# Gathering two heads of a cached page with one indirect transfer, and scoring the new key apart

## The chip, the cores and the metric

The kernel runs on one core of one Trainium2 chip. The metric is device time in microseconds (us) of one execution: the median of three executions, with the lowest and the highest beside it. A reading of 0.2% or less is about what a measurement of this kernel cannot tell from no change.

## The reference, cut to what matters

One layer of a decoder works on 256 prompt tokens and on 8 samples with one new token each. Everything is float32. A projection of 2048 features feeds three branches; the change touches only the third, the attention of the 8 samples over a paged cache.

```python
PAGE_SIZE, PAST_LEN, N_KV, N_HEADS, HEAD_DIM = 128, 256, 4, 16, 128     # two pages for each sample
top_k = min(TOPK_MAX, (PAST_LEN + T) // 4)                              # 64 of 257 keys
pool_k = ck.reshape(-1, N_KV, HEAD_DIM)                                 # cache: page, position, kv head, feature
row = phys * PAGE_SIZE + pc % PAGE_SIZE                                 # phys: from the sample's page table
k_sel = jnp.where(is_past, pool_k[row], take_rows(k, ni))               # the 257th key is the new token's
qg = q.reshape(B, T, N_KV, N_HEADS // N_KV, HEAD_DIM)                   # 4 query heads share a kv head
s = jnp.einsum('btngd,btsnd->btngs', qg, k_sel) * HEAD_DIM ** -0.5
p = jax.nn.softmax(jnp.where(valid, s, -jnp.inf), axis=-1)
o = jnp.einsum('btngs,btsnd->btngd', p, v_sel)
```

The kernel computes the scores of all 257 keys of a sample and adds -1e30 to those that the indexer did not select, which gives the same softmax.

## The kernel before, in words

The 264 tokens are the moving operand of all large products, with features on the partitions. The work is a stream of feature tiles of 128 columns, in the order of a list (`ORDER`): the indexer's key, 4 tiles of k, 4 of v, 8 of the indexer's queries, 16 of `va`, 16 of `q` (one for each query head), 16 of `zc`, and the rest. A tile is 16 blocks of K; each block is three matmuls (L1010, `acc<-hh,wh`, `acc<-hl,wh`, `acc<-hh,wl`), since every float32 operand is carried as two parts, a high and a low one. ScalarE makes the high part of the weights (L157, `wh`), VectorE the low one (L160, `wl`). SyncE loads the weights in units of 512 KB into six buffers.

The order of the instructions on each engine is the order in which the program issues them: there is no scheduler. What follows a tile's product is a generator (`Tasks`): it yields the number of steps until it goes on, and a step is one unit of 24 matmuls of the stream, so a tile has two steps. Each engine takes its own instructions strictly in that order and waits by semaphores for the others.

The attention of the samples for kv head `n` (0 to 3) is `sample(n)`. It is spawned 3 steps after the last of the four query heads that share the kv head, and goes through five places, one step apart: the scores of the 8 samples (L726, `ssP`, 8 matmuls whose result is 32 rows by 257 columns, since a 32-row stretch of the result holds two samples); the softmax; its transposes (L736, `spT`); the product with the values (L746, `soP`, 16 matmuls of 32 x 128); the transpose back (L756, `soT`). In the trace a float32 matmul of this kind is two rows, so `ssP` has 16 and `soP` 32 for each `sample(n)`.

The keys and values come from HBM by indirect transfers that GpSimd issues (`gather`, L711 to L717): one for each sample, page and kv head, of 128 rows of 512 bytes, row numbers from `rows`. There are 16 for the keys and 16 for the values of one kv head, 128 in all. The buffers `gk` and `gv` hold two kv heads each: `top_k` issues the gathers of heads 0 and 1 (keys 0, values 0, keys 1, values 1), `sample(0)` and `sample(1)` issue those of heads 2 and 3 into the places that they have just read. The new token's key is copied into column 256 of `gk` by VectorE (L721).

Of the kernel before, what the change touches and what calls it, by code (L numbers as in the profile page):

```python
# [10 lines left out]
I32 = mybir.dt.int32  # L11
# [20 lines left out]
# first column of each part of w_in  # L32
# [3 lines left out]
# feature tiles of 128 columns in the order in which they are computed  # L36
# [9 lines left out]
# the first tiles are computed in parts of K, while the modulation of the later parts still comes in  # L46
# [3 lines left out]
# buffers of loads; units that are split ahead of their use (one, for the first NEAR loads), each in  # L50
# CUT parts; tiles over which the loads of the next piece's modulation are spread
# [7 lines left out]
def _mods():  # L59
    """The loads of w_mod, by piece of shift and scale or of the gate: columns for each k, the k,  # L60
    and where they are in the packed array."""
    out, off = [], 0
    for width in [256 * nk for _, nk in PIECES] + [128 * nk for _, nk in GATES]:
        per = max(1, 1024 // width)
        out.append([])
        for k in range(0, KB, per):
            out[-1].append((width, list(range(k, k + per)), off))
            off += width * per * P
    return out
# [5 lines left out]
def _stream():  # L75
    """The loads in the order in which they are used: ("m", piece, load) of w_mod, and ("w", n, parts)
    of the tiles' weights, eight blocks of 128 x 128 each, as (tile, first k block, k blocks)."""
    items, n = [("m", 0, i) for i in range(len(MODS[0]))], 0
    for q, (k0, nk) in enumerate(PIECES):
        ms = [("m", q + 1, i) for i in range(len(MODS[q + 1]))] if q + 1 < len(PIECES) else []  # L80
        done = 0
        for j in range(0, EARLY, 8 // nk):
            while done < len(ms) and done * MOD_BY <= j * len(ms):
                items.append(ms[done])
                done += 1
            items.append(("w", n, [(x, k0, nk) for x in range(j, j + 8 // nk)]))
            n += 1
        assert done == len(ms)
    gate = [("m", q, i) for q in range(len(PIECES), len(MODS)) for i in range(len(MODS[q]))]
    for j in range(EARLY, len(ORDER)):  # L90
        for k0 in (0, 8):
            items.append(("w", n, [(j, k0, 8)]))
            n += 1
            if gate and ORDER[j][0] in ("u", "za"):
                items.append(gate.pop(0))
    return items
# [4 lines left out]
# columns of the packed per-feature parameters, [128, KB] each unless said otherwise  # L101
# [4 lines left out]
class Tasks:  # L106
    """Work that follows a tile's product, spread over later steps: generators that yield the
    number of steps until they go on."""
# [21 lines left out]
def trunk_kernel(ctx: ExitStack, tc: tile.TileContext, a: dict, o: dict):  # L130
# [11 lines left out]
    def slot(name, dt=F32, shape=(P, KB, T)):  # L142
        return big.tile(list(shape), dt, name=name, tag="big")
# [28 lines left out]
    # the tensor engine's clock comes up before the first loads arrive  # L172
# [32 lines left out]
    def ctile(name, shape, dt=F32, bufs=1):  # L205
        return cp.tile(list(shape), dt, name=name, tag=name, bufs=bufs)

# [9 lines left out]
    rows = ctile("rows", [P, 5, 16], I32)  # L217
    rowf = ctile("rowf", [P, 16])
    dve.tensor_scalar(rowf, ptf, 128.0, pidx[:, 0:1], op0=OP.mult, op1=OP.add)
    for n in range(4):  # L220
        dve.tensor_scalar(rows[:, n, :], rowf, float(n * N_PHYS * P), None, op0=OP.add)
    dve.tensor_scalar(rows[:, 4, :], ptf, 64.0, pidx[:, 1:2], op0=OP.mult, op1=OP.add)

    # sel[b, r] = 1 where row r = 32 (b // 2) + 4 (b % 2) + h belongs to sample b
# [6 lines left out]
    # heads of the indexer on partitions, 16 b + h: a copy of the identity for each sample  # L231
# [21 lines left out]
    # the extra buffers are for the loads up to the last of shift and scale  # L253
# [27 lines left out]
    # the weights of the next units, up to the n-th from here on, in the two parts that float32r  # L281
    # carries
# [32 lines left out]
    # 1 / sqrt(x / D + EPS), with a step of Newton's behind ScalarE's square root  # L315
# [12 lines left out]
    # the same of the tokens' sums over the partitions, for every partition, in PSUM  # L328
# [36 lines left out]
    # 1 / rms of the tokens, for every partition  # L365
# [25 lines left out]
    # up to four groups of n columns, a tile of 32 columns of the tensor engine's for each  # L391
# [94 lines left out]
    def gather_kix():  # L486
        kix = S["kix"] = slot("kix", shape=(P, NS, KEYS))
        for b in range(NS):
            for g in range(PAGES):
                i = b * PAGES + g  # L490
                pool.indirect_dma_start(out=kix[:, b, g * P:(g + 1) * P], out_offset=None, in_=a["cidx"],
                                        in_offset=bass.IndirectOffsetOnAxis(ap=rows[:, 4, i:i + 1], axis=0))
# [62 lines left out]
    def post_qi(j, src):  # L555
# [5 lines left out]
        # a head's 64 rows in two parts that float32r carries, one above the other  # L561
# [28 lines left out]
    def top_k():  # L590
# [21 lines left out]
        S["gk"] = slot("gk", shape=(P, 2, NS, KEYS))  # L612
        S["gv"] = slot("gv", shape=(P, 2, NS * PAGES, P))
        for n in range(2):
            gather(n, "gk")
            gather(n, "gv")
# [47 lines left out]
    # prompt attention of one head; the samples' after the last head of a group  # L664
    def post_q(h, src):
# [8 lines left out]
        if hh4 == 3:  # L674
            tasks.spawn(sample(n), 3)
# [35 lines left out]
    def gather(n, what):  # L711
        for b in range(NS):
            for g in range(PAGES):
                i = b * PAGES + g
                to = S["gk"][:, n % 2, b, g * P:(g + 1) * P] if what == "gk" else S["gv"][:, n % 2, i, :]
                pool.indirect_dma_start(out=to, out_offset=None, in_=a["ck" if what == "gk" else "cv"],  # L716
                                        in_offset=bass.IndirectOffsetOnAxis(ap=rows[:, n, i:i + 1], axis=0))  # L717

    def sample(n):
        gk, gv = S["gk"], S["gv"]  # L720
        dve.tensor_copy(gk[:, n % 2, :, 256], kT[:, n, NP:T])  # L721
        yield 1
        p = pss("ssP")
        for s in range(2):
            for c in range(4):
                pe.matmul(p[32 * c:32 * c + 32, 0:KEYS], qpad[n % 2][:, c, 32 * s:32 * s + 32],  # L726
                          gk[:, n % 2, 2 * c + s, :], start=s == 0, stop=s == 1, skip_group_check=True)
        if n < 2:
            gather(n + 2, "gk")
# [13 lines left out]
        for s in range(2):  # L743
            for g in range(PAGES):
                for c in range(4):
                    pe.matmul(p[32 * c:32 * c + 32, 0:P], ppad[n % 2][:, g, c, 32 * s:32 * s + 32],  # L746
                              gv[:, n % 2, (2 * c + s) * PAGES + g, :], start=first, stop=s == 1 and g == 1,
                              skip_group_check=True)
                first = False
        if n < 2:  # L750
            gather(n + 2, "gv")
# [22 lines left out]
    # twice silu(z)  # L774
# [24 lines left out]
    # merged holds twice the sum  # L799
# [134 lines left out]
    # what has to be there before a tile's work  # L934
    def start_a():
# [21 lines left out]
        # the part of the samples' convolution that comes from their state  # L957
# [9 lines left out]
    # 4 log(sigmoid(x)) = 4 (min(x, 0) - 2 atanh(y / (2 + y))), y = exp(-|x|)  # L967
# [85 lines left out]
    # the prompt's rows come back to tokens on partitions, where 1 / rms is one factor for each  # L1053
# [40 lines left out]
def _layout(i):  # L1094
# [29 lines left out]
    def feat(x):  # L1124
# [13 lines left out]
        ck=i["cache_k"][0].transpose(2, 0, 3, 1).reshape(-1, P),  # L1138
        cv=i["cache_v"][0].transpose(2, 0, 1, 3).reshape(-1, P),
# [48 lines left out]
```

## Time and profile before

| | us |
|---|---|
| device time, median of 3 | 1746.52 (1745.45 to 1747.11) |
| span of the profiled execution, first to last instruction | 1614.2 |
| what lies around the span, by the median | 132.3 |
| TensorE busy with matmuls | 1578.5 (98% of the span) |
| VectorE, ScalarE, GpSimd busy | 990.1, 807.9, 295.5 |
| TensorE's mean granted clock | 0.990 of full speed |

The profile is of one execution. No device time of its own was kept for that execution, so the median of the three stands for it: 1746.5 = 1614.2 + 132.3. The 132.3 us are outside all the instructions of the program. Where the text speaks of kv head 0 it means the stretch at about 328 to 343 us of the span, of head 1 362 to 382, of head 2 402 to 422, and of head 3 442 to 464.

### The profile page before, as it was taken

Reading aid. Unit: us, or ns where it says so; the run is one execution under the profiler, and the core shown is the slowest. Engines: PE = TensorE matmul, PEld = TensorE weight load, DVE = VectorE, ACT = ScalarE, POOL = GpSimd, SP = SyncE. Lnnn points to the kernel's source line nnn. Section 1 sums busy time; section 2 is a strip of 40 time slices with the busy share of each in tenths; the row PEclk is TensorE's granted clock in tenths of the full one; section 3 lists DMA queues with packets and bytes.
Section 4 is the critical chain, followed back from the end, with each engine's and each line's share of the span. In section 5 each row is a group of like instructions: output and inputs, shape, how many; then the busy total and the mean of one; then the engine's idle time right before and its main releaser. Section 6 shows DMA issues by size and latency. Waiting matters only on the chain.

```text
span 1614.2 us, 33342 instructions
## 1 busy us (share of the span) xinstructions
PE 1578.5 (98%) x13289; PEld 1518.1 (94%) x13289; DVE 990.1 (61%) x2111; ACT 807.9 (50%) x1628; POOL 295.5 (18%) x411
## 2 busy tenths in 40 slices
PE   8999999998889999999999999999999999999998
PEld 7888899998879999998889999999999999999997
DVE  6876589754446645544546654444777777766654
ACT  5333368554435444443334444444777777754442
POOL 4000256577730001000000000000211111100011
PEclk9999999999989999999999999999999999999999
DMA  8898863655445555657885556555465545555652
GB/s 337 304 362 286 284 207 119 192 180 155 156 151 174 185 182 184 201 184 268 286 273 186 172 182 235 181 181 181 152 198 174 173 162 186 180 190 183 234 183 83
DMA packets 91867, 326.26 MB, mean 202 GB/s; under 512 B 12320, under 2 KB 12768, under 8 KB 91328
## 3 DMA queue, kind: packets, MB, share of 16 engines
q1 hardware_dynamic: 86608, 313.18, 57.4%
q0 software_dynamic: 5104, 10.96, 2.3%
q8 instruction: 104, 1.70, 0.4%
q14 instruction: 51, 0.42, 0.1%
HBM read 320.35 MB, written 3.67 MB: 201 GB/s over the span
## 4 chain that ended last, share of the span: by engine, by line
PE 70%; DVE 1%; issue 0%; POOL 0%; DMA 0%; ACT 0%; DVEq 0%; ACTq 0%
PE acc L1010 68%; PE pmod L407 1%; PE spP L838 0%; PE giP L879 0%; PE gaP L879 0%; POOL gv L716 0%; DVE x L161 0%; DVE ls L158 0%; DMA gv<-in_cv,rows 0%; DVE ls L981 0%; DVE wl L160 0%; PE rsP L1063 0%; DVE o L158 0%; DVEq L1154 0%; ACT wh L157 0%
## 5 line engine op out<-in xcount | busy, mean ns | idle before, releaser
L160 DVE TENSOR_TENSOR wl<-raw,wh 128x512 fp32r<-128x512 f32 x926 | 613.2, 706 | 371.9 <-ACT wh L157 352.8
L1010 PE MATMUL acc<-hh,wh 128*128 128x264 f32 x2832 | 822.5, 290 | 6.8 <-DVE part L159 2.6
L1010 PE MATMUL acc<-hh,wl 128*128 128x264 f32 x2832 | 805.1, 284 | 1.9 <-DVE wl L160 1.9
L1010 PE MATMUL acc<-hl,wh 128*128 128x264 f32 x2832 | 806.0, 285 | 0.1
L157 ACT ACTIVATE wh<-raw 128x512 fp32r<-128x512 f32 x926 | 530.3, 622 | 496.6 <-PE acc L1010 357.4
L1010 PEld LDWEIGHTS acc<-hh,wh 128*128 128x128 f32 x2832 | 536.6, 189 | 41.0 <-issue 25.1
L1010 PEld LDWEIGHTS acc<-hl,wh 128*128 128x128 f32 x2832 | 537.0, 190 | 0.7 <-DVE hl L160 0.4
L1010 PEld LDWEIGHTS acc<-hh,wl 128*128 128x128 f32 x2832 | 534.2, 189 | 2.3 <-DVE wl L160 2.3
L1010 PE MATMUL acc<-ah,wh 128*128 128x264 f32 x768 | 217.9, 284 | 0.0
L1010 PE MATMUL acc<-al,wh 128*128 128x264 f32 x768 | 217.6, 283 | 0.0
L1010 PE MATMUL acc<-ah,wl 128*128 128x264 f32 x768 | 217.4, 283 | 0.0
L1010 PEld LDWEIGHTS acc<-al,wh 128*128 128x128 f32 x768 | 144.7, 188 | 0.0
L1010 PEld LDWEIGHTS acc<-ah,wh 128*128 128x128 f32 x768 | 144.6, 188 | 0.0
L1010 PEld LDWEIGHTS acc<-ah,wl 128*128 128x128 f32 x768 | 144.0, 187 | 0.0
L810 POOL TENSOR_TENSOR mg<-mg,gp 128x264 f32<-128x264 f32 x16 | 12.0, 752 | 473.8 <-DVE gp L161 473.8
L159 DVE TENSOR_TENSOR part<-acc,part 128x264 f32<-128x264 f32 x128 | 51.6, 428 | 35.6 <-PE acc L1010 35.2
L1010 PE MATMUL acc<-mh,wh 128*128 128x264 f32 x256 | 72.6, 284 | 0.0
L1010 PE MATMUL acc<-ml,wh 128*128 128x264 f32 x256 | 72.5, 283 | 0.0
L1010 PE MATMUL acc<-mh,wl 128*128 128x264 f32 x256 | 72.5, 283 | 0.0
L716 POOL DMA_INDIRECT gk<-in_ck,rows x64 | 64.2, 1003 | 19.4 <-issue 16.3
L716 POOL DMA_INDIRECT gv<-in_cv,rows x64 | 62.1, 970 | 19.5 <-issue 18.3
L1010 PEld LDWEIGHTS acc<-ml,wh 128*128 128x128 f32 x256 | 48.2, 188 | 0.0
(377 smaller groups left out, 1266.8 us busy)
## 6 DMA issues: line engine op xcount, KB each, us to landing
raw<-in_wall SPq DMA_DIRECT2D x463, 512.0 KB, 3.7
raw<-in_wmod SPq DMA_DIRECT2D x73, 512.0 KB, 5.6
rawx<-in_wmod SPq DMA_DIRECT2D x23, 512.0 KB, 6.4
rawx<-in_wall SPq DMA_DIRECT2D x19, 512.0 KB, 6.0
xr<-in_xT SPq DMA_DIRECT2D x4, 528.0 KB, 5.6
wrg<-in_wrg SPq DMA_DIRECT2D x1, 2048.0 KB, 8.5
x<-in_xp SPq DMA_DIRECT2D x1, 2048.0 KB, 9.5
out_yp<-x SPq DMA_DIRECT2D x8, 256.0 KB, 2.4
```

The lines of the kernel that those rows point to most:

```text
L157: copy = lambda out, x, scale=1.0: act.activation(out, x, AF.Copy, scale=scale)
L159: add = lambda out, x, y: dve.tensor_tensor(out, x, y, OP.add)
L160: sub = lambda out, x, y: dve.tensor_tensor(out, x, y, OP.subtract)
L407: pe.matmul(MOD[q][32 * g:32 * g + 32, 0:n], cpad[:, k, :], r[:, c:c + n], start=k == 0, stop=k == KB - 1, skip_group_check=True)
L716: pool.indirect_dma_start(out=to, out_offset=None, in_=a["ck" if what == "gk" else "cv"], in_offset=bass.IndirectOffsetOnAxis(ap=rows[:, n ...
L810: pool.tensor_tensor(S["mg"][:, j, :], S["mg"][:, j, :], x, OP.add)
L1010: pe.matmul(c[:, 0:T], x[:, kk * P:(kk + 1) * P], y[:, k, :], start=n == 0 and (kk == 0 if early else k == 0), stop=n == 2 and (kk == nk - ...
```

## The change

One transfer now fetches both kv heads of a pair for a page: 128 rows of 1,024 bytes, for which the host lays out the caches with the two heads of a pair side by side. There are 16 gathers for the keys and 16 for the values of a pair, 64 in all. `gk` and `gv` hold one pair; `top_k` issues the gathers of pair 0 (heads 0 and 1), and `sample(1)` issues those of pair 1 (heads 2 and 3), the keys behind its scores and the values behind its product. The scores of the cached keys are matmuls of 256 columns; the new token's key no longer goes into `gk`, and its column of scores comes from 8 matmuls of one column for each kv head (32 more in all). `sample(2)` starts 5 steps behind its query head and no longer 3. Two of the five tables of row numbers go.

```diff
@@ indexer and attention: constants
-    rows = ctile("rows", [P, 5, 16], I32)
+    rows = ctile("rows", [P, 3, 16], I32)
...
-    for n in range(4):
-        dve.tensor_scalar(rows[:, n, :], rowf, float(n * N_PHYS * P), None, op0=OP.add)
+    for n in range(2):
+        dve.tensor_scalar(rows[:, n, :], rowf, 2.0, float(n), op0=OP.mult, op1=OP.add)
@@ top_k
-        S["gk"] = slot("gk", shape=(P, 2, NS, KEYS))
-        S["gv"] = slot("gv", shape=(P, 2, NS * PAGES, P))
-        for n in range(2):
-            gather(n, "gk")
-            gather(n, "gv")
+        S["gk"] = slot("gk", shape=(P, NS * PAGES, 2, P))
+        S["gv"] = slot("gv", shape=(P, NS * PAGES, 2, P))
+        gather(0, "gk")
+        gather(0, "gv")
@@ post_q
-            tasks.spawn(sample(n), 3)
+            tasks.spawn(sample(n), 5 if n == 2 else 3)
@@ gather, sample
-    def gather(n, what):
-        for b in range(NS):
-            for g in range(PAGES):
-                i = b * PAGES + g
-                to = S["gk"][:, n % 2, b, g * P:(g + 1) * P] if what == "gk" else S["gv"][:, n % 2, i, :]
-                pool.indirect_dma_start(out=to, out_offset=None, in_=a["ck" if what == "gk" else "cv"],
-                                        in_offset=bass.IndirectOffsetOnAxis(ap=rows[:, n, i:i + 1], axis=0))
+    def gather(pair, what):
+        for i in range(NS * PAGES):
+            pool.indirect_dma_start(out=S[what][:, i].rearrange("p n x -> p (n x)"), out_offset=None,
+                                    in_=a["ck" if what == "gk" else "cv"],
+                                    in_offset=bass.IndirectOffsetOnAxis(ap=rows[:, pair, i:i + 1], axis=0))
 
     def sample(n):
         gk, gv = S["gk"], S["gv"]
-        dve.tensor_copy(gk[:, n % 2, :, 256], kT[:, n, NP:T])
+        h = n % 2
         yield 1
         p = pss("ssP")
         for s in range(2):
             for c in range(4):
-                pe.matmul(p[32 * c:32 * c + 32, 0:KEYS], qpad[n % 2][:, c, 32 * s:32 * s + 32],
-                          gk[:, n % 2, 2 * c + s, :], start=s == 0, stop=s == 1, skip_group_check=True)
-        if n < 2:
-            gather(n + 2, "gk")
+                b = 2 * c + s
+                pe.matmul(p[32 * c:32 * c + 32, 0:NP], qpad[n % 2][:, c, 32 * s:32 * s + 32],
+                          gk[:, PAGES * b:PAGES * b + PAGES, h, :], start=s == 0, stop=s == 1,
+                          skip_group_check=True)
+        for s in range(2):
+            for c in range(4):
+                b = NP + 2 * c + s
+                pe.matmul(p[32 * c:32 * c + 32, NP:KEYS], qpad[n % 2][:, c, 32 * s:32 * s + 32],
+                          kT[:, n, b:b + 1], start=False, stop=s == 1, skip_group_check=True)
+        if n == 1:
+            gather(1, "gk")
...
-                              gv[:, n % 2, (2 * c + s) * PAGES + g, :], start=first, stop=s == 1 and g == 1,
+                              gv[:, (2 * c + s) * PAGES + g, h, :], start=first, stop=s == 1 and g == 1,
...
-        if n < 2:
-            gather(n + 2, "gv")
+        if n == 1:
+            gather(1, "gv")
@@ _layout (on the host)
-        ck=i["cache_k"][0].transpose(2, 0, 3, 1).reshape(-1, P),
-        cv=i["cache_v"][0].transpose(2, 0, 1, 3).reshape(-1, P),
+        ck=i["cache_k"][0].transpose(0, 3, 2, 1).reshape(-1, 2 * P),
+        cv=i["cache_v"][0].reshape(-1, 2 * P),
```

The change also takes the comments out of the file, which shifts the line numbers by a few.

On GpSimd's queue, from the last work on the mask of the prompt (`bias`) to the store of `gv` rows at the end of the gMLP's norm (`out_gv`), the rows before are these, 16 gathers to a row:

```order
L588 AFFINE_SELECT bias<-bias 128x256
L716 DMA gk<-in_ck,rows 128x128 x16
L716 DMA gv<-in_cv,rows 128x128 x16
L716 DMA gk<-in_ck,rows 128x128 x16
L716 DMA gv<-in_cv,rows 128x128 x16
L716 DMA gk<-in_ck,rows 128x128 x16
L716 DMA gv<-in_cv,rows 128x128 x16
L716 DMA gk<-in_ck,rows 128x128 x16
L716 DMA gv<-in_cv,rows 128x128 x16
L662 DMA out_gv<-vsr 128x128
```

and now:

```order
L589 AFFINE_SELECT bias<-bias 128x128
L590 AFFINE_SELECT bias<-bias 128x256
L715 DMA gk<-in_ck,rows 128x256 x16
L715 DMA gv<-in_cv,rows 128x256 x16
L715 DMA gk<-in_ck,rows 128x256 x16
L715 DMA gv<-in_cv,rows 128x256 x16
L663 DMA out_gv<-vsr 128x128
```

The values of head 1, which stood behind 48 other gathers, now come with those of head 0, behind 16; the last gather of all stands behind 63 others and no longer 127.

On TensorE's queue, the scores of kv head 0 (`ssP`), between the transposes of a query head of the prompt (`pT`) and the stream's next matmul (`acc`), were:

```order
L691 MATMUL oP<-et,vn 128x256
L693 MATMUL oP<-et,vn 128x128
L686 MATMUL pT<-ident,e 128x128 x3
L726 MATMUL ssP<-gk,qpad_169 32x257 x8
L1010 MATMUL acc<-hh,wh 128x264
```

and are now:

```order
L692 MATMUL oP<-et,vn 128x256
L694 MATMUL oP<-et,vn 128x128
L687 MATMUL pT<-ident,e 128x128 x3
L727 MATMUL ssP<-gk,qpad_167 32x256 x8
L733 MATMUL ssP<-kT,qpad_167 32x1 x8
L1017 MATMUL acc<-hh,wh 128x264
```

The eight matmuls of one column stand directly behind the eight of the cached keys; the same holds for the other three kv heads.

On TensorE's queue, the first nine rows of the product with the values of kv head 1 (`soP`) with the semaphores that they wait for (DMASW0 to DMASW7 are eight counters of GpSimd's transfers, taken in turn) were:

```order
L679 MATMUL sP<-kT,qt 128x256
L746 MATMUL soP<-gv,ppad_172 32x128 [waits DMASW6_49,DVE_49]
L746 MATMUL soP<-gv,ppad_172 32x128 [waits DMASW2_49]
L746 MATMUL soP<-gv,ppad_172 32x128 [waits DMASW6_49]
L746 MATMUL soP<-gv,ppad_172 32x128 [waits DMASW2_49]
L746 MATMUL soP<-gv,ppad_172 32x128 [waits DMASW7_49]
L746 MATMUL soP<-gv,ppad_172 32x128 [waits DMASW3_49]
L746 MATMUL soP<-gv,ppad_172 32x128 [waits DMASW7_49]
L746 MATMUL soP<-gv,ppad_172 32x128 [waits DMASW3_49]
L746 MATMUL soP<-gv,ppad_172 32x128 [waits DMASW0_49,DVE_49]
```

and all sixteen of them now are:

```order
L680 MATMUL sP<-kT,qt 128x256
L753 MATMUL soP<-gv,ppad_170 32x128 [waits DVE_49]
L753 MATMUL soP<-gv,ppad_170 32x128 x7
L753 MATMUL soP<-gv,ppad_170 32x128 [waits DVE_49]
L753 MATMUL soP<-gv,ppad_170 32x128 x7
L1017 MATMUL acc<-hh,wh 128x264
```

The products of heads 1 and 3 wait for no transfer of their own any more, since heads 0 and 2 have already waited for the same gathers.

## Rows read from the trace of the kernel before

**Rows 1.** The head of the page: the span, and each engine's busy time with its share of the span.

```profile
span 1614.2 us, 33342 instructions
PE 1578.5 (98%) x13289; PEld 1518.1 (94%) x13289; DVE 990.1 (61%) x2111; ACT 807.9 (50%) x1628; POOL 295.5 (18%) x411
```

**Rows 2.** TensorE's waits between 296 and 470 us: who waited for what, us in total, times, longest.

```profile
PE soP L746 <- DMA gv<-in_cv,rows: 15.3, 8, 5.0
```

**Rows 3.** TensorE's timeline at the four products with the values: start us, length us (of the whole run where there are several), line, operation, count, and in brackets the idle time before it with what ended it. First kv head 0, then 1, 2 and 3; each ends with the stream's first matmul behind the product, and with the first one that was started at the old pace again (the 18th, 19th and 14th from there).

```profile
341.37 1.08 PE L746 MATMUL soP<-gv,ppad 128*32 128x128 f32 x32
342.38 0.39 PE L1010 MATMUL acc<-hh,wh 128*128 128x264 f32 x1
342.60 0.28 PE L1010 MATMUL acc<-hl,wh 128*128 128x264 f32 x1
...
374.58 0.42 PE L746 MATMUL soP<-gv,ppad 128*32 128x128 f32 x6
...
381.12 0.59 PE L1010 MATMUL acc<-hh,wh 128*128 128x264 f32 x1
...
385.09 0.29 PE L1010 MATMUL acc<-hh,wh 128*128 128x264 f32 x1
...
415.05 0.42 PE L746 MATMUL soP<-gv,ppad 128*32 128x128 f32 x6
...
421.59 0.59 PE L1010 MATMUL acc<-hh,wh 128*128 128x264 f32 x1
...
425.91 0.29 PE L1010 MATMUL acc<-hl,wh 128*128 128x264 f32 x1
...
453.08 0.57 PE L746 MATMUL soP<-gv,ppad 128*32 128x128 f32 x6
458.70 0.66 PE L746 MATMUL soP<-gv,ppad 128*32 128x128 f32 x8 [5.05 <-DMA gv<-in_cv,rows]
...
463.67 0.59 PE L1010 MATMUL acc<-hh,wh 128*128 128x264 f32 x1
...
466.88 0.28 PE L1010 MATMUL acc<-hh,wl 128*128 128x264 f32 x1
```

**Rows 4.** The chain of work that ended last, in order of time (start us, length us, what): the end of the gathers and the stretch of TensorE behind them.

```profile
458.71 0.94 POOL gv L716
...
459.96 3.10 DMA gv<-in_cv,rows
...
468.38 52.21 PE acc L1010 x432
```

**Rows 5.** Busy time of each engine in stretches (us from the span's start, length, busy time and count of PE, PEld, DVE, ACT and POOL, TensorE's granted clock, share of the DMA engines, GB/s): two microseconds around the product of head 1, and the whole stretch of the gathers.

```profile
379.00:380.00 1.00, 0.68 (x13) 0.62 (x16) 0.00 (x0) 0.00 (x0) 0.69 (x2) 0.50 0.29 70
385.00:386.00 1.00, 1.00 (x10) 1.00 (x9) 0.00 (x0) 0.00 (x0) 0.70 (x2) 1.00 0.79 315
...
296.00:464.00 168.00, 151.81 (x1241) 139.15 (x1240) 87.05 (x306) 76.22 (x198) 126.20 (x128) 0.94 0.53 167
```

**Rows 6.** GpSimd's timeline: the first and the last gather of the keys of head 0, the last of the values of head 0, the first of the keys of head 1, the first of the keys of head 2, and the last of all.

```profile
295.93 1.40 POOL L716 DMA_INDIRECT gk<-in_ck,rows  x1 [0.16 <-issue]
...
316.44 0.94 POOL L716 DMA_INDIRECT gk<-in_ck,rows  x1 [0.30 <-issue]
...
337.15 0.94 POOL L716 DMA_INDIRECT gv<-in_cv,rows  x1 [0.30 <-issue]
338.39 0.94 POOL L716 DMA_INDIRECT gk<-in_ck,rows  x1 [0.30 <-issue]
...
379.32 0.94 POOL L716 DMA_INDIRECT gk<-in_ck,rows  x1 [0.31 <-issue]
...
459.96 0.94 POOL L716 DMA_INDIRECT gv<-in_cv,rows  x1 [0.30 <-issue]
```

**Rows 7.** TensorE's timeline at the scores of kv heads 0 and 1, with the stream's next matmul.

```profile
328.56 1.08 PE L726 MATMUL ssP<-gk,qpad 128*32 128x257 f32 x16
329.56 0.39 PE L1010 MATMUL acc<-hh,wh 128*128 128x264 f32 x1
...
361.80 1.08 PE L726 MATMUL ssP<-gk,qpad 128*32 128x257 f32 x16
362.81 0.39 PE L1010 MATMUL acc<-hh,wh 128*128 128x264 f32 x1
```

**Rows 8.** The costliest groups of GpSimd that issue transfers: line, operation, tiles, count, busy us, mean ns of one, idle before them. `out_h` has 128 rows of 576 bytes (16 tiles of 9 floats), `out_k` 128 rows of 4,224 bytes (4 tiles of 264).

```profile
L716 POOL DMA_INDIRECT gv<-in_cv,rows x64 | 62.1, 970 | 19.5 <-issue 18.3 <-PE ssP L726 0.6 <-DMA gv<-in_cv,rows 0.3
L534 POOL DMA_DIRECT2D out_k<-kT x1 | 0.6, 587 | 4.1 <-ACT kT L157 4.1
L906 POOL DMA_DIRECT2D out_h<-hout x1 | 0.5, 537 | 0.0
```

**Rows 9.** Transfers: tiles, queue, kind, count, KB of one, and the median time in us from issue to landing.

```profile
raw<-in_wall SPq DMA_DIRECT2D x463, 512.0 KB, 3.7
gk<-in_ck,rows POOLq DMA_INDIRECT x64, 2.7
gv<-in_cv,rows POOLq DMA_INDIRECT x64, 3.2
```

**Rows 10.** Instructions by one line, with the shortest, the median and the longest duration in ns: matmuls of one column (the gMLP's norm), and the copy of the new key.

```profile
L651 PE MATMUL vnP<-ones,sqacc x4: 166/250/250, 520.4 to 520.7; 128*128 128x1 f32 x4
L721 DVE COPY gk<-kT x4: 202/204/298, 325.1 to 440.6; 128x8 f32<-128x8 f32 x4
```

More of the change, by code (lines that the diff above doesn't have):

```diff
@@ L216, in trunk_kernel @@
     pool.iota(pidx[64:P, 1:2], pattern=[[0, 1]], base=0, channel_multiplier=1, allow_small_or_imprecise_dtypes=True)
-    rows = ctile("rows", [P, 5, 16], I32)
+    rows = ctile("rows", [P, 3, 16], I32)
     rowf = ctile("rowf", [P, 16])
     dve.tensor_scalar(rowf, ptf, 128.0, pidx[:, 0:1], op0=OP.mult, op1=OP.add)
-    for n in range(4):
-        dve.tensor_scalar(rows[:, n, :], rowf, float(n * N_PHYS * P), None, op0=OP.add)
-    dve.tensor_scalar(rows[:, 4, :], ptf, 64.0, pidx[:, 1:2], op0=OP.mult, op1=OP.add)
+    for n in range(2):
+        dve.tensor_scalar(rows[:, n, :], rowf, 2.0, float(n), op0=OP.mult, op1=OP.add)
+    dve.tensor_scalar(rows[:, 2, :], ptf, 64.0, pidx[:, 1:2], op0=OP.mult, op1=OP.add)
     sli = ctile("sli", [NS, 32], I32)
@@ L491, in gather_kix @@
                 pool.indirect_dma_start(out=kix[:, b, g * P:(g + 1) * P], out_offset=None, in_=a["cidx"],
-                                        in_offset=bass.IndirectOffsetOnAxis(ap=rows[:, 4, i:i + 1], axis=0))
+                                        in_offset=bass.IndirectOffsetOnAxis(ap=rows[:, 2, i:i + 1], axis=0))
     kT = ctile("kT", [P, 4, T])
```

## The prediction, made before the changed kernel ran

> **What bounds the kernel now.** I read the head of the page first [rows 1]: TensorE is busy for 98% of the span, the others for 18% to 61%. So time can only go where TensorE waits or runs slowly, or where it gets more work. The second view is therefore TensorE's own waits, and of these the ones in the stretch of the gathers: one line, 15.3 us in 8 waits, all of the product with the values (`soP`) for transfers into `gv` [rows 2]. The chain of work that ended last runs through the same place: gather after gather on GpSimd, the landing of the last one (3.10 us), and then TensorE alone [rows 4]. So GpSimd, idle for 82% of the span, sets the pace for a moment: it issues 128 gathers without a gap from 295.93 to 459.96 us [rows 6], one every 164.03 / 127 = 1.29 us, while TensorE reaches the four products at 341, 375, 415 and 453 us [rows 3].
>
> The third view tells what that costs, which is more than the idle time. The product of head 0 waits for nothing: 341.37 to 342.38, 1.01 us. The same work takes 381.12 - 374.58 = 6.54 us for head 1, 421.59 - 415.05 = 6.54 for head 2 and 463.67 - 453.08 = 10.59 for head 3 [rows 3]. Beyond 1.01 each that is 5.53 + 5.53 + 9.58 = **20.6 us**. Behind each wait the stream is slow for a while: the granted clock is 0.50 (the lower level, 1.2 GHz) where the product ends and 1.00 (2.4 GHz) again at 385 us [rows 5]. The pace at the full clock is 52.21 / 432 = 0.121 us a matmul [rows 4], and 0.22 for the first one behind a product (342.38 to 342.60). 18 matmuls then take 2.28 us, and took 3.97; 19 take 2.40, and took 4.32; 14 take 1.79, and took 3.21 [rows 3]: **5.0 us** more. These waits and their tails hold 25.7 us.
>
> **The change part by part.**
>
> *Half as many gathers.* GpSimd issues 32 (keys and values of pair 0), is then held until the scores of head 1 are done, and issues 32 more. The question is when each value lands and when TensorE asks for it. The first 32 gathers stand where they stood, 295.93 to 337.15, 41.22 / 31 = 1.33 us apart [rows 6].
> - Head 0: the last value gather starts at 337.15 and lands 3.2 us later by the median [rows 9], at 340.4. The rows that read it are the last of a product that begins at 341.37 or later, so they run at about 342.4, and at 342.9 with the half microsecond below. It stays free, by 2.5 us.
> - Head 1: its values come with those of head 0. No wait is left: 5.53 + 1.69 = 7.2 us gone.
> - Head 2: the keys of pair 1 may be issued when the scores of head 1 are done, at 362.8 [rows 7] plus two heads' new matmuls, 363.8. 31 steps of 1.33 later the last value gather starts, at 405.0, and lands at 408.2. The queue's second condition, that head 1's product has read the old values, is met by then (about 377, while GpSimd comes to the values at 385). The product of head 2 began at 415.05; it moves 7.2 earlier with head 1's wait, 1.5 later by new matmuls, and two steps later by the new delay. Two steps are a tile, and four tiles lie between the scores of heads 0 and 1: (361.80 - 328.56) / 4 = 8.3, some 7.5 without the samples' own share. So it begins at 416.9 and asks for the last value at 417.9: free by 9.7 us, and by 2.2 without the new delay. Its scores stand 12.8 us ahead of it, at 404, and their keys have landed by 387. 5.53 + 1.92 = 7.45 us gone.
> - Head 3: it shares these transfers and comes later still. 9.58 + 1.42 = 11.0 us gone.
>
> Behind the held gathers GpSimd's queue has only the store `out_gv`, for which nobody waits.
>
> *What a gather of 1,024-byte rows costs.* The trace has none. What GpSimd spends on a transfer of 128 rows hardly depends on the row: 537 ns with 576 bytes, 587 with 4,224 [rows 8], 50 ns for 3,648 bytes more, so 7 ns for 512 more; 32 times that is 0.2 us and lies inside the free 2.5. The other bound is that the work doubles with the bytes, 970 ns more [rows 8], which is a rival below. I take the rows: +0. For the landing the bounds are the 2.7 to 3.2 us of 64 KB and the 3.7 us of a 512 KB load [rows 9]; 128 KB lies between, at most 0.5 later than I used, also inside the free 2.5. The Trainium skill ("DMA: Bandwidth & Descriptors", section on the anatomy of one SWDGE DMA) fits such a transfer as about 2.0 us plus bytes / 436e3: 2.15 us for 64 KB and 2.30 for 128 KB by that estimate. The rows are slower than that fit by half a microsecond or more; its growth of 0.15 us would be hidden too.
>
> *The new key's column.* 8 matmuls more for each head, 16 rows in the trace, 64 in all, on the engine that is full, so all of it counts. The nearest row is `soP`: the same 128 x 32 weights and a short moving operand, 32 rows in 1.01 us, 0.032 each [rows 3]: 64 x 0.032 = **2.0 us**. The scores' own rows, with twice the columns, take 1.00 / 16 = 0.0625 [rows 7], so 4.0 us; rows of one column, but with weights four times as wide, are about 0.1 apart [rows 10], so 6.4 us. Below, the new rows could hide in the gaps of their neighbours: 0. I take 2.0, since these weights are loaded as in `soP`. The Trainium skill ("TensorE: Matmul & The Clock Gate", section on 56 ns against 53.3 ns) gives a floor of about 25 ns between starts however small a matmul is, and about 62 ns where the sequencer decodes in software: 1.6 or 4.0 us here. The trace's 32 ns speak against the second.
>
> *At nothing:* 256 columns in place of 257; VectorE's four copies of 204 ns [rows 10] and two row tables less, on an engine at 61% [rows 1]. If VectorE were the bound, that would be 0.8 us gained.
>
> **The sum.** -20.6 - 5.0 + 2.0 = -23.7 us. The span of 1614.2 becomes 1590.5. The profiled execution has no device time of its own; with the 132.3 us around the span, by the median of the runs, the forecast is **1722.8 us**, 1.4% less.
>
> **The rivals.**
> - *The bigger gather is somewhat slower to issue.* Per gather x us more, the last value of head 0 lands 32x later and has 2.5 us free: from x = 0.08 on head 0 waits, and then pays a slow tail of 1.7. At x = 0.25 that is 8.0 - 2.5 + 1.7 = 7.2, so 1730. For it: the shortest gathers, all of one size, can't exclude it. Against it: [rows 8].
> - *Gathering costs by the byte (slower).* With x = 0.97 head 0 waits 31.0 - 2.5 = 28.5 (some 5 of it at its scores), with two tails of 1.7, 31.9 in all; head 2 waits 31.0 - 9.7 = 21.3 plus 1.9. Then 1746.5 - 23.7 + 55.1 = 1778. It decides from 64x = 23.7 + 2.5 - 1.7 + 9.7 - 1.9 on, x = 0.5, a gather of about 1.5 us. Against it: the two direct transfers above.
> - *Another bound steps in.* The same loads and splits must fit into 144 us where they had 168 [rows 5]: the DMA share goes from 0.53 to 0.62, VectorE from 52% to 60%, ScalarE from 45% to 53%. None is near its end, and the only line of TensorE's waits there is the gathers' [rows 2]. If half the gain went: 1735.
> - *Nothing happens,* if recording the profile slowed GpSimd's queue and the timed executions never waited: then only the 2.0 us are left, 1748. Nothing in the rows speaks for it.
>
> **How the numbers follow.** All three waits gone: 0.78 (1720.8 to 1727.2 by the bounds of the new matmuls). Somewhat slower gathers 0.07, another bound 0.07, cost by the byte 0.05, nothing 0.03. The range reaches from 1719 (no cost of the new matmuls, and the spread of the runs below it) to 1731 (the dearest new matmuls, or x = 0.25), and leaves out less than 2 in 10. Faster by over 0.2% (3.5 us, about what a measurement tells from no change): 0.93; within it 0.02; slower 0.05.
>
> **What the profile after would show.** TensorE's waits without a line of `soP` for `gv`; the four products 1.0 us each and a granted clock of 1.00 from 330 to 460 us; 64 gathers at the old 0.94 us, in two runs of 32 with GpSimd idle between; 64 rows of one column, about 0.5 us for each head. A line of `soP` at about 343 us would mean that the gather has grown; one at 417, that pair 1 comes too late; a `wl` or `wh` line, that a new bound has come in.

## The result, and the profile after

The changed kernel took 1674.63 us (median of 4 runs, 1674.20 to 1676.12) beside 1746.82 us (4 runs) of the kernel before: a ratio of 0.9587, 95% interval 0.9574 to 0.9600, or 72.2 us less. The forecast was 23.7 us less, 1722.8, with 1719 as the low end. The change did three times what was predicted.

Both kernels have two levels of time, each of which held for all runs of a session (the runs made one after the other on one chip): the kernel before takes 1615 to 1620 us in a **calm** session and 1745 to 1750 us in a **stalling** one. The result is from a stalling session; the profile of before [rows 1] is of a calm execution (1614.2 us), which I couldn't know, but could have suspected.

The head of the profile after, the tenths of the span (40 slices of 42 us) and, in the last lines, TensorE's longest waits:

```profile
span 1672.5 us, 33369 instructions
PE 1596.7 (95%) x13353; PEld 1530.6 (92%) x13353; DVE 988.4 (59%) x2105; ACT 809.0 (48%) x1628; POOL 231.5 (14%) x347
PE   8999899859699999999999999999999999999997
POOL 4000327521500000000000000000112112100011
PEclk9999899869789999999999999999999999999999
q8 instruction: 105, 1.72, 0.4%
```
```profile
PE acc L1017 <- issue: 26.5, 34, 2.2
PE sP L679 <- ACT qt L157: 14.3, 1, 14.3
PE pT L687 <- issue: 4.0, 4, 1.7
```

The profiled execution took 1674.2 us for a span of 1672.5, so only 1.7 us lie around the span. The 132.3 us that the table of times before puts outside all instructions are a difference between two unlike executions. The waits of [rows 2] are gone: no line has `soP` for `gv`. In their place stand lines that the profile before did not have, behind `issue`: the engine waited for nothing that the profile shows. Between the first and the last slice, TensorE's digits fall below 9 in slices 4, 7, 8 and 10 (counted from 0) alone, which are the stretches in which GpSimd gathers (188 to 208, 310 to 350, 411 to 462 us).

What such a stretch looks like, on TensorE's timeline (start, length, what, idle time before it), 9 us behind the first gather of pair 0 (309.69 us):

```profile
318.61 0.28 PE L1017 MATMUL acc<-hh,wl 128*128 128x264 f32 x1
318.73 0.38 PE L687 MATMUL pT<-ident,e 128*128 128x128 f32 x2
319.27 0.27 PE L687 MATMUL pT<-ident,e 128*128 128x128 f32 x1 [0.16 <-issue]
320.01 0.36 PE L1017 MATMUL acc<-hh,wh 128*128 128x264 f32 x1 [0.47 <-issue]
320.21 0.28 PE L1017 MATMUL acc<-hl,wh 128*128 128x264 f32 x1
320.70 0.28 PE L1017 MATMUL acc<-hh,wl 128*128 128x264 f32 x1 [0.21 <-issue]
321.43 0.39 PE L1017 MATMUL acc<-hh,wh 128*128 128x264 f32 x1 [0.44 <-issue]
321.65 0.28 PE L1017 MATMUL acc<-hl,wh 128*128 128x264 f32 x1
322.85 0.38 PE L1017 MATMUL acc<-hh,wl 128*128 128x264 f32 x1 [0.91 <-issue]
```

Up to 318.7 the stream runs at its 0.12 us a matmul; then starts stand 0.7 us or twice that apart, over and over, in front of matmuls of the plain stream that have nothing to wait for. ScalarE fares worse: one copy (`et`) came after 28.5 us of idle time that is put down to `issue`, and TensorE's 14.3 us for `qt` are that copy's successor.

```profile
348.30 0.49 ACT L157 ACTIVATE et<-pT 128x384 f32<-128x384 f32 x1 [28.51 <-issue]
```

### The profile page after: what moved, and what is told of

Read it like the earlier page. It is cut to its first block, busy times and chain, and to the rows that moved or that the text cites. A ratio compares the mean times of both kernels' runs of the same rounds, so it can differ in the third digit from the quotient of the medians.

```text
span 1672.5 us, 33369 instructions
## 1 busy us (share of the span) xinstructions
PE 1596.7 (95%) x13353; PEld 1530.6 (92%) x13353; DVE 988.4 (59%) x2105; ACT 809.0 (48%) x1628; POOL 231.5 (14%) x347
## 3 DMA queue, kind: packets, MB, share of 16 engines
q0 software_dynamic: 4080, 10.95, 2.3%
q8 instruction: 105, 1.72, 0.4%
## 4 chain that ended last, share of the span: by engine, by line
PE 89%; issue 3%; DVE 3%; another core or an unknown queue 2%; DMA 2%; ACT 1%; SPq 0%; DVEq 0%; ACTq 0%
PE acc L1017 82%; PE pmod L409 3%; DVE wl L160 1%; DMA raw<-in_wall 1%; ACT wh L157 1%; PE oP L692 0%; PE spP L845 0%; DMA xr<-in_xT 0%; PE sP L680 0%; PE giP L886 0%; PE gaP L886 0%; DVE part L159 0%; PE pT L687 0%; PE soP L753 0%
## 5 line engine op out<-in xcount | busy, mean ns | idle before, releaser
L409 PE MATMUL pmod<-raw,cpad 128*32 128x256 f32 (+1 forms) x672 | 50.2, 360 | 2.7 <-issue 2.5
L1017 PEld LDWEIGHTS acc<-mh,wh 128*128 128x128 f32 x256 | 48.2, 188 | 0.0
```

What stands on the lines that cost most here:

```text
L409: pe.matmul(MOD[q][32 * g:32 * g + 32, 0:n], cpad[:, k, :], r[:, c:c + n], start=k == 0, stop=k == KB - 1, skip_group_check=True)
L1017: pe.matmul(c[:, 0:T], x[:, kk * P:(kk + 1) * P], y[:, k, :], start=n == 0 and (kk == 0 if early else k == 0), stop=n == 2 and (kk == nk - ...
```

## The experiments

**1. Is the time around the span, or in it? Do gathers, bytes or their queue matter?** Four kernels in one session:

```
before_again: the kernel before, unchanged
no_kv:       gather():  - pool.indirect_dma_start(...)   + if pair == 0: pool.memset(S[what], 0.5)
half_bytes:  gather():  in_= rows of 128 columns, out=S[what][:, i, 0]; sample(): h = 0
plain_pool:  gather():  + pool.dma_start(S[what][:, i], <page i, pair>)   # 64, same bytes
```

> The kernel before once more, now with the span of the very execution that is timed. Theory G (while GpSimd issues indirect gathers, the other engines' sequencers are short of instructions, about 1 us lost for each gather, 144 of them): the span is about 1745 us, only 2 us lie around it, and TensorE idles for some 110 to 130 us more than in the profile shown before, in the two stretches with gathers and behind `issue`. Rival O (132 us of launch work lie outside the span, as the prediction took it): span 1614, time 1747, no such idle time.

> The changed kernel without its 64 gathers of keys and values (both caches filled with a constant by GpSimd, so heads' cache data are left out). Theory G: all stalls of the stretch 309 to 463 us go, some 64 us: about 1610 us; what is left over is the stall at the 16 indexer gathers. Rival S (the stalls come with something else in that stretch, instruction volume or the table loads of ScalarE): 1665 to 1675.

> The changed kernel with as many gathers, each of 512-byte rows (64 KB) in place of 1,024; the second head of a pair reads the first one's data, so half of the cache is left out. Theory G, by the number of gathers: the same as after, 1670 to 1676. Rival B, by the bytes that GpSimd's queue moves: half of the loss of 64 us goes, about 1642.

> The changed kernel with the 64 indirect gathers turned into 64 plain transfers of GpSimd's queue, same place, same bytes and rows, from fixed pages (so the page table is left out). Theory G in its narrow form, only indirect transfers stall the others: about 1612. In its wide form, any transfer whose descriptors GpSimd makes: 1640 to 1675, by the time that GpSimd spends on one (0.54 to 0.59 against 0.95 us).

Measured: the kernel before 1616.11 (span 1614.4) and, as the reference of the session, 1618.91; `no_kv` 1592.77, `half_bytes` 1592.22, `plain_pool` 1595.02. The session was calm, so both theories on the kernel before missed: not 132 us outside the span, and no stall in it either; it simply took 130 us less than in the recorded runs. The times forecast for the three variants missed with them. All three cost the same within 3 us, so here nothing of the gathers shows.

**2. The change itself in a calm session, and the price of the new key.** Both kernels were timed in several rounds; the second repeats the matmuls of the new key:

```
newkey_x4: sample():  + for rep4 in range(4):        # around the eight matmuls of the new key
```

> The changed kernel once more, timed against the kernel before. Theory C (the same kernel takes 1616 to 1619 us on one chip and 1747 on another, and what is added there lies in the gathers): where the kernel before takes 1616 to 1619, this one takes 1592 to 1594, a ratio of 0.985, as the prediction's sum of -23.7 has it, and TensorE has no idle time behind `issue` in the stretches with gathers; where the kernel before takes 1747, it takes 1675. Rival W (gathers of 1,024-byte rows stall the other engines by themselves, those of 512 bytes don't): 1675 also where the kernel before takes 1617, so slower than it by 3.5%.

> The changed kernel with the eight matmuls of the new key issued four times for each head, so 192 more in all (the new key's score counts four times, which changes that key's weight). By the prediction's price, 0.032 us each: +6.1 us against the changed kernel on the same chip. By the other bounds: +12 us at 0.0625, +19 at 0.1, and 0 if they hide in the gaps of their neighbours.

Measured: 1593.34 us (4 runs) beside 1616.98 (7 runs), ratio 0.9850 (0.9833 to 0.9866): **23.6 us less, where the sum said 23.7**, and a span of 1591.4, where it said 1590.5. The interval reaches from 21.7 to 27.0 us less, so the agreement to 0.1 us is luck. Rival W falls. `newkey_x4` took 1595.60 (1593.80 to 1597.62), 2.3 us more for 192 rows, some 0.012 us each, under half of the 0.032 that was taken. The trace of `after_again` (first three lines, kv head 1: scores, new key, the stream's next) and of `newkey_x4` (head 0) agree:

```profile
362.21 1.07 PE L727 MATMUL ssP<-gk,qpad 128*32 128x256 f32 x16
363.09 0.28 PE L733 MATMUL ssP<-kT,qpad 128*32 128x1 f32 x16
363.31 0.39 PE L1017 MATMUL acc<-hh,wh 128*128 128x264 f32 x1
```
```profile
331.72 0.97 PE L734 MATMUL ssP<-kT,qpad 128*32 128x1 f32 x64
332.62 0.39 PE L1018 MATMUL acc<-hh,wh 128*128 128x264 f32 x1
```

16 rows of the new key take 363.31 - 363.09 = 0.22 us, 64 rows 0.90: 0.014 each. And the scores themselves, from their start to that of the next row, take 0.88 us where [rows 7] had about 1.00.

**3. A version without indirect gathers.** If gathering is what stalls, page numbers can be read into SyncE's registers and the pages fetched by its plain loads:

```
reg_pages:   + page = [nc.values_load(pti[0:1, i:i+1], engines=[SP], ...) for i in range(16)]
             gather():      + sp.dma_start(S[what][:, i], src[ds(page[i], 1), :, pair, :])
             sample():      pair 1's loads spawned 4 steps later
             gather_kix():  + 2 x sp.dma_start(kix[half], keys[ds(page[i], 1)]) for each page
reg_pages2:  gather_kix() as a task, one page (read, two loads) for each step of the stream
reg_pages2_b, reg_pages3: reg_pages2 again
```

> The changed kernel without any indirect gather: SyncE reads the 16 page numbers into registers and issues 64 plain loads of 128 KB for keys and values and 32 of 32 KB for the indexer's keys from its own queue (those of pair 1 two tiles later than the gathers were). Theory C (the gathers are what a disturbed chip stretches): beside a kernel before of 1747 us it takes 1590 to 1600 us; beside one of 1617 it takes what the changed kernel takes, 1590 to 1596, as there the gathers are hidden. Rival D (what is disturbed is the chip as a whole, its clock or its memory): beside 1747 it takes 1670 or more, like the changed kernel. Rival Q (SyncE's queue is held up by the new loads and the weights come late): 1600 to 1620 on either chip, with waits of TensorE for `wl` or `wh`.

> As reg_pages, but SyncE reads one page number and issues the two indexer loads of that page per step of the stream, in place of 16 reads at the very start and 32 loads in a row. By reg_pages' own waits (6.0 us at the start, 9.4 us behind the 32 loads) most of its 15 us over the changed kernel should go: 1591 to 1597 beside a kernel before of 1617. Theory C: also 1591 to 1600 beside a kernel before of 1747. Rival D (the whole chip is disturbed there): 1670 or more beside 1747.

> The same kernel without indirect gathers (SyncE's plain loads by page numbers in registers). Theory C (GpSimd's gathers are what is stretched on a chip where the kernel before takes 1747): 1588 to 1592 on either kind of chip. Rival D (such a chip is disturbed as a whole): 1640 or more where the kernel before takes 1747.

> The kernel without indirect gathers (page numbers in SyncE's registers, plain loads, two of the indexer's per step), timed in three rounds. Theory C: 1588 to 1592, so a ratio of 0.911 beside a kernel before of 1747 and of 0.984 beside one of 1617, with a spread no wider than that of the others.

Measured: `reg_pages` 1608.39 beside 1616.54 (calm): rival Q's time, but not its waits, for two others had the loss:

```profile
PE wiP L528 <- ACT wiT L157: 9.4, 1, 9.4
PE pmod L412 <- DVE sqacc L159: 6.0, 1, 6.0
```

Spread over the steps, `reg_pages2` took 1589.98 beside 1617.11 and, timed, 1590.70 (4 runs) beside 1617.87, ratio 0.9838 (0.9822 to 0.9855): in a calm session no different from the change, within the intervals. In a stalling one it took **1591.18 beside 1746.16**, a ratio of 0.911, where the change took 1674.63 (in another stalling session). Rival D falls: what stalls there is not the chip as a whole, but what the gathers touch. Windows of that execution (stretch, its length, busy time and count of PE, PEld, DVE, ACT, POOL, granted clock, DMA share, GB/s):

```profile
185.00:300.00 115.00, 113.72 (x938) 107.87 (x938) 94.19 (x232) 75.82 (x166) 47.05 (x92) 1.00 0.56 184
300.00:480.00 180.00, 179.12 (x1605) 171.75 (x1604) 110.14 (x347) 94.78 (x237) 0.00 (x0) 1.00 0.57 186
```

**4. Number or bytes, indirect or plain, in a stalling session.** `split128` undoes one part of the change alone, the size of the gathers; the other two are those of the first session:

```
split128: gather():  for h in range(2): pool.indirect_dma_start(out=S[what][:, i, h], in_=src of 128 columns, ...)
```

> The changed kernel with each gather of 1,024-byte rows cut into two of 512, so 128 gathers again with the same bytes, still whole pairs and the new key by matmuls. Beside a kernel before of 1617 (no stretching of the gathers): the values of a pair now land some 41 us later than in the changed kernel, so the waits of `soP` or `ssP` for the caches come back, by name, 20 to 60 us of them: 1610 to 1650. Beside a kernel before of 1747: if the disturbance goes by the number of gathers, 0.9 us for each, another 58 us on top; if it goes by the bytes or by each stretch with gathers, nothing on top of the named waits.

> Once more the kernel with 64 plain transfers on GpSimd's queue in place of the indirect gathers of keys and values (fixed pages). Beside a kernel before of 1747: if only indirect transfers stretch the stretch they are in, 1595 plus the share of the 16 indexer gathers, some 8 to 16 us: 1603 to 1611; if every transfer whose descriptors GpSimd makes does so, about 1 us for each, like the changed kernel: 1655 to 1680. Beside 1617: 1593 to 1596 as before.

> Once more 64 gathers of 512-byte rows (half of the cache left out). Beside a kernel before of 1747: by the number of gathers 1670 to 1676, like the changed kernel; by the bytes 1640 to 1645. Beside 1617: 1590 to 1594.

Measured, beside 1748.83, 1745.74 and 1745.74 (the bytes: GpSimd's queue moved 10.95 MB in the changed kernel and 1.51 without gathers; a cache is 4.2, the indexer 1.0):

| kernel | indirect gathers | MB gathered by them | calm us | stalling us | lost us |
|---|---|---|---|---|---|
| before | 128 + 16 | 9.4 | 1616.98 | 1746.82 | 129.8 |
| after | 64 + 16 | 9.4 | 1593.34 | 1674.63 | 81.3 |
| `half_bytes` | 64 + 16 | 5.2 | 1592.22 | 1674.09 | 81.9 |
| `split128` | 128 + 16 | 9.4 | not met | 1757.42 | |
| `plain_pool` | 16 | 1.0 | 1595.02 | 1608.02 | 13.0 |
| `reg_pages2` | 0 | 0 | 1590.70 | 1591.18 | 0.5 |

The stalling values of the last four rows are single runs (`half_bytes2`, `split128`, `plain_pool2`, `reg_pages2_b`), and so are the calm ones of `half_bytes` and `plain_pool`; the calm one of `reg_pages2` is `reg_pages3`. The counts are those of keys and values and, behind the plus, of the indexer.

Half the bytes at the same number loses the same; twice the number at the same bytes (`split128` against after) costs 82.8 us more, so that the whole gain of the change is gone (1757.42 beside 1748.83; why it is 9 us over the kernel before is not shown); 64 plain transfers of GpSimd's own queue lose nothing, since the 13.0 us are those of the indexer's 16 gathers. The first line below is the stretch of the 64 plain transfers in `plain_pool2`, as full of matmuls as in `reg_pages2_b`; the second is `split128`'s longest wait:

```profile
300.00:480.00 180.00, 179.12 (x1603) 171.69 (x1602) 110.18 (x357) 94.43 (x235) 36.62 (x68) 1.00 0.58 190
```
```profile
PE acc L1018 <- issue: 82.5, 60, 2.4
```

So the loss goes by the number of indirect gathers (all have 128 rows, so the number of gathers and that of rows are not told apart), and the change gains by having 64 fewer. The 129.8 us of the kernel before are net: its calm time holds the 25.7 us of waits and tails that a stalling execution does not have, so its stalls cost some 155 us, an estimate. `split128` had none of the waits for the caches that I expected by name: TensorE was late enough itself.

**5. From the first gather on?** In the stalling traces TensorE's first delayed start stands 8.6 to 10.3 us behind the first gather of the indexer's burst and of the first one for keys, which is some seven or eight gathers; behind later bursts it is 5.7 to 11.6 us.

```
kix8: plain_pool, and in gather_kix(): indirect for i < 8, two pool.dma_start of fixed pages for the other 8
```

> The kernel with plain transfers of GpSimd for keys and values, and now with indirect gathers for 8 of the 16 indexer pages only; the other 8 come by 16 plain transfers of GpSimd from fixed pages. So a single burst of 8 indirect gathers is left. Beside a kernel before of 1747: if each gather costs its share from the first on, half of the 13 us that 16 of them cost there: 1601 to 1603, with TensorE's gaps of 0.7 us or its multiples from about 190 us on; if the first eight or so of a burst are free, as the start of the gaps 9 to 10 us behind the first gather suggests, 1594 to 1597 and no such gaps.

> The same kernel again (8 indirect gathers in one burst, all other transfers plain). Beside a kernel before of 1747: 1601 to 1603 with TensorE's gaps of 0.7 us or its multiples from about 190 us on, if each gather pays from the first on; 1594 to 1597 without such gaps, if the first eight of a burst are free. Beside a kernel before of 1617: 1593 to 1597, which tells nothing between them.

The first try told nothing: a calm session, and an execution in which the stream's matmuls took 510 to 514 ns by the mean in place of 284 to 290, all through, at a granted clock of 1.00 (3616.75 us; nothing in the kernel accounts for it, and the next run of the session was as usual). The second met a stalling session, 1745.74: **1596.01**. The stretch of the indexer's gathers, with 16 of them (`plain_pool2`) and with 8 (`kix8_b`):

```profile
185.00:300.00 115.00, 106.53 (x824) 98.61 (x823) 84.14 (x202) 68.06 (x151) 60.23 (x104) 0.94 0.47 157
```
```profile
185.00:300.00 115.00, 113.59 (x935) 107.54 (x934) 92.60 (x225) 75.59 (x166) 65.49 (x120) 1.00 0.56 182
```

935 matmuls fit where 824 did, and TensorE's waits have no line behind `issue` any more. So in this one execution a single burst of eight is free, and the second eight cost the 13 us. A gather has no fixed price.

**6. The kernel before where it takes 1747.**

> The kernel before, for a profile on a chip where it takes 1747 us. Theory C: span 1743 to 1747, with 100 us or more of TensorE's idle time behind `issue` or behind engines that are themselves short of instructions, all of it between the tenth gather of the indexer and the last gather of the values, and little or no wait of `soP` for `gv` left, since TensorE is late itself. Rival O: span 1614 and the rest outside. Beside 1617 it tells nothing new.

> As the last one: the kernel before, for a profile on a chip where it takes 1747 us. Theory C: span 1743 to 1747, 100 us or more of TensorE's idle time in the stretches with gathers, behind `issue` or behind engines that are themselves short of instructions, and little or no wait of `soP` for `gv`. Rival O: span 1614 and the rest outside.

The first met a calm session (1617.17, span 1615.5). The second did not: 1745.91, span 1744.2, on a chip of the same number as in the first session, which was calm. The head of its page, TensorE's longest waits, and two windows (the indexer's gathers; the 128 others, 311 to 536 us, and what follows them):

```profile
span 1744.2 us, 33342 instructions
PE   8999899517558999999999999999999999999998
POOL 4000345672442000000000000000022111110011
q8 instruction: 104, 1.70, 0.4%
```
```profile
PE acc L1010 <- issue: 65.9, 51, 2.4
PE spT L736 <- ACT oc L157: 24.5, 2, 12.9
PE sP L678 <- issue: 13.8, 1, 13.8
```
```profile
185.00:290.00 105.00, 95.89 (x736) 87.04 (x735) 74.15 (x175) 59.43 (x132) 53.91 (x95) 0.93 0.47 155
290.00:560.00 270.00, 157.28 (x1084) 143.13 (x1083) 83.10 (x285) 73.01 (x184) 132.58 (x142) 0.75 0.32 98
```

No wait of `soP` for `gv` is left in this execution: TensorE comes late itself, and the values are there.

## Why the prediction was wrong, point by point

- **The failed step is the last line of the sum**: "with the 132.3 us around the span". The runs show 1.7 us around the span (1674.2 against 1672.5; 1745.91 against 1744.2). The 132 us were in the span of the timed executions, as stalls in the stretches with gathers, which the change about halves (148 us to 71, below). A constant carried over from one execution to another was taken for time outside the kernel, with no row behind it.
- **The cause at the level of the result is another one.** In a stalling session the waits of [rows 2], the source of the 25.7 us, do not exist, so they cannot be gained. In the 270 us above TensorE did 1084 matmuls, which at the 176 us for 1570 of a calm execution of the changed kernel (290 to 466 us) take 121.5 (an estimate): 148 us lost there. After, the stretch of 300 to 480 us holds 972 in 180 us, 109 us of work: 71 lost.

```profile
300.00:480.00 180.00, 134.10 (x972) 121.20 (x971) 69.01 (x245) 61.31 (x157) 64.19 (x68) 0.80 0.43 132
```
```profile
290.00:466.00 176.00, 175.12 (x1570) 167.70 (x1569) 108.97 (x354) 91.78 (x231) 64.80 (x66) 1.00 0.56 189
```

  The difference, some 77 us, is about the measured 72; the indexer's gathers stall in both. (The first of the two windows is of the changed kernel's stalling execution, the second of its calm one.) The sign of a granted clock of 1.00 failed there: 0.80.
- **Waits and slow tails gone, 25.7 us: right, in a calm session.** The products of `after_again` start at 341.77, 375.06 and 415.80 (416.9 was forecast for the third) and take 1.0 us each; no `gv` line is left; the granted clock is 1.00 from 290 to 466 us.
- **A gather of 1,024-byte rows costs no more to issue: right,** 946 ns by the median beside 944, also in a stalling session (0.95). Pair 1 went nearly as forecast, which had 363.8 and 405.0:

```profile
363.10 0.94 POOL L715 DMA_INDIRECT gk<-in_ck,rows  x1 [24.66 <-PE ssP L727]
403.06 0.95 POOL L715 DMA_INDIRECT gv<-in_cv,rows  x1 [0.30 <-PE pT L687]
```

- **The landing of a bigger gather: mis-sized, without effect.** The forecast had 3.2 us for the values and at most 0.5 more. Those of `after_again` took:

```profile
DMA to landing us min/median/max: 3.0/4.5/5.8
```

  The last value gather of pair 0 starts at 337.49 and lands, by that median, at 342.0, while the product of head 0 ends at about 342.8. So 0.8 us were free, not 2.5: that head 0 does not wait came out right by a narrow margin.
- **The new key, +2.0 us: mis-sized.** It is 4 x 0.22 = 0.9 us, and the scores in front of it give 4 x 0.12 = 0.5 back (by the column less, or by what follows them: not shown). Rows of one column behind 32-column weights, 0.014 us each, go faster than the 128-column rows of `soP`, 0.032, the nearest row that I took, and faster than the floor of 25 ns that the prediction quotes (here the measurement decides); the two errors are under the noise of a timed run.
- **The rivals.** None of the four held. "Nothing happens" came nearest in kind: it asked whether recording and timing could be of different executions, but only with the recording as the slower one.

## What to carry to other kernels

Before a sum is made against a trace, put the trace's span beside the times. Here 1.7 us lay around a span; the 132 us meant that the trace was of an execution unlike the timed ones, and the first question was which stretch is longer there, not what lies around it. Price a change of indirect gathers by their number and by how many stand in one burst, as well as by the waits for their data. Where another engine can issue the same pages as plain loads by page numbers in registers, spread over the steps of the stream (all at once they cost 15 us), that is as fast as the change in a calm session and, in a stalling one, 155 us of 1746 less than the kernel before.

## What the runs showed of the hardware that I had not expected

- In some sessions, long bursts of indirect gathers on GpSimd (0.95 us each, 1.25 us apart) hold up the other engines, which then wait for nothing that the profile shows: starts of TensorE 0.7 us or multiples of it apart, ScalarE idle for 28.5 us, while GpSimd's own gathers take what they always take. Eight in a burst cost nothing, the next eight 13 us, 64 + 16 some 81, 128 + 16 some 130, net of the waits that vanish. Plain transfers of the same queue, and SyncE's loads, do nothing of the kind.
- What the engines lack is not shown. The Trainium skill ("Runtime: NRT & Kernel Launch", section on instruction fetch mechanics) says that each engine's sequencer fetches its instructions in 16 KiB blocks through a DMA queue of its own, ahead of use, so that the fetch is mostly hidden. The traces have these blocks (`q8`, 105 packets and 1.72 MB, in the calm and in the stalling execution of the changed kernel alike), and no packet of it that is slow: the longest takes 1.52 us in the stalling execution, 1.81 in the calm one. Late blocks alone cannot be what TensorE's gaps wait for. From 315 to 363 us the stalling execution moves no block of `q8`, and TensorE starts 108 matmuls in it all the same, gap after gap; a gap that ends without a block arriving did not wait for that arrival. The calm execution moves four blocks and starts 425 matmuls in that stretch, so the blocks come in step with TensorE's rows in both. The window of the stalling execution and its queues, then those of the calm one:

```profile
315.00:363.00 48.00, 22.94 (x108) 18.73 (x108) 13.09 (x44) 6.86 (x17) 26.92 (x28) 0.61 0.42 124
q0 software_dynamic: 1417, 3.85, 29.3%
q1 hardware_dynamic: 576, 2.10, 12.3%
q14 instruction: 1, 0.01, 0.1%
```
```profile
315.00:363.00 48.00, 47.71 (x425) 44.71 (x428) 27.30 (x99) 25.83 (x69) 18.21 (x18) 1.00 0.57 192
q8 instruction: 4, 0.07, 0.6%
```

  What holds the engines up stays open, as does what makes a session a stalling one; a chip of one number was met in both kinds.
